# A hybrid decoder step on one core: where the extra weight slots live, and the order of two sets of output projections

## The chip, the cores and the metric

The kernel runs on one core of a Trainium2 chip. The metric is the device time of one execution in microseconds. The median of three runs before the change is 1149.12 us (1148.29 to 1151.05). The engines are called as in the profile: PE is the matmul engine and PEld its weight load, DVE the vector engine, ACT the scalar engine, POOL the GpSimd engine, and SP the queue that issues most transfers.

## The reference, cut to what matters

Two layers of a decoder run on 512 prompt tokens and 8 sampled tokens, all in float32:

```
for i in range(2):
    if i == 0:  m = attention(x)      # q,k,v projection, sliding window 128, sinks, then @ w_o
    else:       m = gated_linear_attention(x)   # q,k,v,gate, 4 heads, then @ w_o
    x = layer_norm(ALPHA * x + m)
    h = x @ w_up[i]; a, u = halves of h
    y = (gelu(causal_conv3(a)) * u) @ w_down[i]
    x = layer_norm(ALPHA * x + y)
```

Beside x, the kernel returns the new key and value windows, the new GLA states (for each of the 8 samples and 4 heads a 128x256 matrix, decayed and updated with an outer product), and the new convolution rows.

## The kernel before, in words

**Groups and units.** The 520 tokens are two groups: A has 256 columns, B has 264 (256 prompt and the 8 samples). All activations lie transposed, features on the partitions. The weights are cut into 187 units of up to 128 output columns (`plan`): 10 for q, k, v; 8 for the attention's output projection; 68 for the first feed-forward (44 up, 24 down in three parts); 25 for the GLA (a rank-16 projection and six per head); 8 for its output projection; 68 for the second feed-forward. So there are six phases, in this order. Each unit is used twice, once for A and once for B. Such a use is called a product here, and A3 is the product of group A with the fourth unit of the phase at hand.

**Precision.** A float32 product is made of three reduced-precision ones. `load_unit` (L147) brings a unit in with one DMA into `raw` (two buffers), ACT copies it into a high part `wh` (L158), DVE subtracts to get the low part `wl` (L161). `product` (L164) then runs 24 matmuls: for each of eight 128-row chunks `wh` times the activations' high part, `wh` times their low part, and `wl` times the high part. In most of the feed-forward, group A uses a wider form with the same work (`product2`, L178). Products are summed in four PSUM buffers (`accp`).

**Slots.** `wh` and `wl` live in slots. Six are there all the time (`WSLOTS`). When B has used a unit, its slot takes the next unit that is not yet loaded (`next_unit`), so a unit that takes over a slot can't be converted before that B product has read the old one. One more slot (`EXTRA`) is a pool of its own. It is opened when a feed-forward begins and closed near its end; it takes no new unit among the last eight of a layer (`XEND`). Pools lie on a stack: a pool that is opened takes the memory of the pools closed before it.

**Order.** `order` gives the program order of products. A runs ahead of B, by a number of products from `LEADS`. In the output projections it gives

```
layer 0   A0 A1 A2 A3 A4 A5 B0 A6 B1 B2 A7 B3 B4 B5 B6 B7
layer 1   A0 A1 A2 A3 A4 B0 A5 B1 A6 B2 A7 B3 B4 B5 B6 B7
```

and a feed-forward begins A0 to A5, B0, A6, B1, B2, A7, B3, A8, B4, and so on in turn, and ends A67, B63, B64, B65, B66, B67. That is program order. The order on each engine is made by a scheduler, which runs the program in a timing model of its own and gives each engine what is ready there, earlier work first. `issue_after` and `keep_in_program_order` add edges that fix the order of two instructions on one engine.

**After a product.** An output projection adds its result to x (L219) and feeds the running sums of a layer norm (`ln_chunk`). Behind the eighth, `ln_end` finishes the norm: column sums by matmuls with `ones_a` (L256), a few rows of statistics on DVE and ACT, eight subtractions of the mean, most on POOL (L263), and then for each chunk a multiplication on DVE (`u`, L296), the high part on ACT (L297), x itself on POOL (L298), and the low part on DVE (L301). The next phase's products of this group read these parts.

**The mixers' ends.** Sampled tokens have steps of their own, spawned with a delay counted in products (`spawn`, `due`). `attn_sample` ends three products after B9 of the attention, and closes the attention's pool. `gla_sample` for the last head starts its state updates five products after that head's last value product: four steps, one product apart, each with a DMA that spreads two rows of v over all partitions (`vb`, L840, one buffer), two ACT multiplications (L844), two DVE updates (L845) and a DMA that writes the state out (L846). In program order the last of them stands nine products after that value product, at A5 of the output projection, and there the GLA's pool is closed. The next pool's tiles are `sconv`, `aext` and others of the feed-forward (`ffn_open`), or those of the GLA (`gla_open`).

Of the kernel before, what the change touches and what calls it, by code (L numbers as in the profile page):

```python
# [37 lines left out]


LAG = 4  # L40
LEADS = (4, 5, 5, 5, 4, 5)

WSLOTS = 6
RAWS = 2
HIACT = 2

EXTRA = 1
XEND = 8
ACCS = 4

WARM = 8
# [40 lines left out]
class Net:  # L92
    def __init__(self, tc, ctx, I, O):
# [38 lines left out]
            g.hl = self.act.tile(s, F32R, name=f"hl_{g.name}")  # L132
        self.units = []
        self.w = {}


    def open(self, name, bufs=1):
# [26 lines left out]
    def product(self, g, u, rh, rl):  # L164
        nc = self.nc
        h, l = self.w[u]
        nt = self.units[u][1]
        ps = self.acc.tile([P, 512], F32, name="accp")
        o = ps[:, :g.n].rearrange("p (j t) -> p j t", t=2)
        for k in range(nt):  # L170
            ks = slice(k * P, (k + 1) * P)
            xh, xl = in_turn(rh[:, k]), in_turn(rl[:, k])
            nc.tensor.matmul(o, h[:, ks], xh, start=k == 0, stop=False)  # L173
            nc.tensor.matmul(o, h[:, ks], xl, start=False, stop=False)  # L174
            nc.tensor.matmul(o, l[:, ks], xh, start=False, stop=k == nt - 1)  # L175
        return ps[:, :g.n]

    def product2(self, g, u, rs, rh, rl, wide):  # L178
# [320 lines left out]
    def attn_sample(self, g):  # L499
# [27 lines left out]
        for v in range(2):  # L527
            own = slice(64 * v, 64 * v + 64)
            src = pv[own, :P].rearrange("p (b h) -> p h b", h=16)[:, 8 * v:8 * v + 8]
            for t in range(2):  # L530
                self.split(g.hh[own, :, t, P:], g.hl[own, :, t, P:], src[:, :, t::2])
        self.close(self.ap_cm)


    def out_proj(self, g, u, m, i):
# [5 lines left out]

    def ffn_open(self, layer):
        nc = self.nc
        if EXTRA:
            self.wx, self.wx_cm = self.open(f"wts{layer}", EXTRA)
        self.fp, self.fp_cm = self.open(f"ffn{layer}")
        p = self.fp
        self.sconv = p.tile([P, NF, NS, 2], F32, name="sconv")
# [256 lines left out]
    def gla_sample(self, g, h, q, k, v0, v1, ep, kraw):  # L805
# [42 lines left out]
                g.st.append(self.state_load(h + 1, p))  # L848
        if h == GH - 1:
            self.close(self.gp_cm)  # L850

    def gla_g(self, g, u, h, i):
        nc, n = self.nc, g.n
# [77 lines left out]
    def order(self):  # L931

        out, n = [], len(self.units)
        for p0, p1, top in zip(self.phases, self.phases[1:] + [n], LEADS):
            b = p0
            for u in range(p0, p1):
                out.append((0, u))
                lead = max(LAG, min(top, p0 + 2 * top - u))
                if u < LAG:
                    lead = LAG - 1  # L940
                while b <= u - lead:
                    out.append((1, b))
                    b += 1
            out += [(1, u) for u in range(b, p1)]
        return out

    def more(self, u):

        end = self.phases[3] if u < self.phases[3] else len(self.units)
        return self.nu < end - XEND  # L950

    def next_unit(self, extra):
        u = self.nu
# [6 lines left out]
    def run(self):  # L960
        nc = self.nc
        self.plan()
        self.nu, self.extra, self.close_wx = WSLOTS, {}, False
        self.attn_open()
        self.later, self.slot, self.seq, self.pool_mark = [], 0, 0, None
        for i, u in self.order():
            g = self.groups[i]
            _, _, f, a, pre = self.units[u]
            if i == 0 and pre:
                pre()  # L970
                if pre != self.gla_open:
                    for _ in range(EXTRA):
                        self.next_unit(True)
            self.slot += 1
            self.resume(f(g, u, *a))
            if i == 1:
                x = self.extra.pop(u, False)
                if not x or self.more(u):
                    self.next_unit(x)
                elif not self.extra:  # L980
                    self.close_wx = True
            if self.close_wx and self.fp is None:
                self.close(self.wx_cm)
                self.close_wx = False
            self.due()
        while self.later:
            self.slot += 1
            self.due()
# [115 lines left out]
```

## Time and profile before

| | |
|---|---|
| median of the runs | 1149.12 us (1148.29 to 1151.05) |
| profiled execution | 1146.73 us, of which the span from first to last instruction is 1144.7 us |
| PE, PEld busy | 1104.2 us (96%), 1055.2 us (92%) |
| DVE, ACT, POOL busy | 794.5 us (69%), 575.6 us (50%), 326.4 us (29%) |
| DMA | 122.82 MB, mean 107 GB/s |
| mean granted PE clock | 0.992 of full |

The phases lie about so in the span: attention to 133 us, its output projection mostly to 168 us, first feed-forward to 529 us, GLA to 734 us, its output projection to 767 us, second feed-forward to 1129 us, and the last norm and the output to the end. An instruction's row in the timeline has its start, its length, engine and line, what it writes and reads, its shape, and in brackets the engine's idle time before it with what ended it. A row of windows has for each engine its busy time and, in brackets, its instructions, then the granted clock, the DMA's share and its rate.

### The profile page before, as it was taken

Reading aid. Unit: us, or ns where it says so; the run is one execution under the profiler, and the core shown is the slowest. Engines: PE = TensorE matmul, PEld = TensorE weight load, DVE = VectorE, ACT = ScalarE, POOL = GpSimd, SP = SyncE. Lnnn points to the kernel's source line nnn. Section 1 sums busy time; section 2 is a strip of 40 time slices with the busy share of each in tenths; the row PEclk is TensorE's granted clock in tenths of the full one; section 3 lists DMA queues with packets and bytes.
Section 4 is the critical chain, followed back from the end, with each engine's and each line's share of the span. In section 5 each row is a group of like instructions: output and inputs, shape, how many; then the busy total and the mean of one; then the engine's idle time right before and its main releaser. Section 6 shows DMA issues by size and latency. Waiting matters only on the chain.

```text
span 1144.7 us, 22953 instructions
## 1 busy us (share of the span) xinstructions
PE 1104.2 (96%) x8806; PEld 1055.2 (92%) x8806; DVE 794.5 (69%) x1663; ACT 575.6 (50%) x1253; POOL 326.4 (29%) x556
## 2 busy tenths in 40 slices
PE   8999899999999999999899999989999999999995
PEld 8997798999999999998899999888999999999994
DVE  7897589655665566668867777799655665566657
ACT  5677457534553245435545556456524553245433
POOL 4575568100110011357300101287100110011344
PEclk9999999999999999999899999999999999999998
DMA  7553031323323233243124355341333232232222
GB/s 241 149 183 90 13 111 56 111 93 123 99 93 111 92 99 105 74 133 110 38 89 147 117 177 162 133 145 62 105 96 127 93 106 98 92 111 93 74 63 75
DMA packets 53789, 122.82 MB, mean 107 GB/s; under 512 B 6792, under 2 KB 27312, under 8 KB 53680
## 3 DMA queue, kind: packets, MB, share of 16 engines
q1 hardware_dynamic: 51664, 119.61, 32.4%
q10 hardware_dynamic: 2016, 1.75, 0.5%
q8 instruction: 69, 1.13, 0.4%
q14 instruction: 40, 0.33, 0.1%
HBM read 108.67 MB, written 8.47 MB: 102 GB/s over the span
## 4 chain that ended last, share of the span: by engine, by line
PE 70%; DVE 12%; DMA 6%; ACT 4%; POOL 4%; issue 4%; SPq 0%; ACTq 0%; DVEq 0%; POOLq 0%
PE accp L191 15%; PE accp L174 14%; PE accp L173 14%; PE accp L175 14%; PE accp L192 8%; DMA vb<-dv 3%; DVE wl L161 2%; POOL x_b L298 1%; DVE sgla L845 1%; DMA qs<-hl 1%; ACT wh L158 1%; POOL x_a L298 1%; DVE u L296 1%; PE pv L494 1%; DVE msq L276 1%
## 5 line engine op out<-in xcount | busy, mean ns | idle before, releaser
L161 DVE TENSOR_TENSOR wl<-raw,wh 128x1024 fp32r<-128x1024 f32 (+2 forms) x189 | 231.4, 1226 | 106.7 <-ACT wh L158 105.2
L158 ACT ACTIVATE wh<-raw 128x1024 fp32r<-128x1024 f32 (+2 forms) x185 | 191.9, 1037 | 215.0 <-PE accp L174 196.8
L173 PE MATMUL accp<-xh_b,wh 128*128 128x264 f32 x976 | 271.7, 279 | 2.5 <-DVE hprod L600 2.5
L174 PE MATMUL accp<-xl_b,wh 128*128 128x264 f32 x976 | 271.3, 278 | 0.2
L175 PE MATMUL accp<-xh_b,wl 128*128 128x264 f32 x976 | 270.8, 278 | 0.0
L191 PE MATMUL accp<-xs_a,wh 128*128 128x512 f32 x576 | 196.3, 382 | 0.0
L173 PEld LDWEIGHTS accp<-xh_b,wh 128*128 128x128 f32 x976 | 185.0, 190 | 3.5 <-DVE hprod L600 2.9
L174 PEld LDWEIGHTS accp<-xl_b,wh 128*128 128x128 f32 x976 | 184.9, 189 | 3.1 <-DVE xl_b L301 0.6
L175 PEld LDWEIGHTS accp<-xh_b,wl 128*128 128x128 f32 x976 | 184.8, 189 | 0.8 <-issue 0.6
L192 PE MATMUL accp<-xs_a,wl 128*128 128x256 f32 x576 | 145.4, 273 | 0.0
L173 PE MATMUL accp<-hh_b,wh 128*128 128x264 f32 x480 | 133.7, 279 | 3.3 <-ACT hh_b L198 3.3
L174 PE MATMUL accp<-hl_b,wh 128*128 128x264 f32 x480 | 134.3, 280 | 0.0
L175 PE MATMUL accp<-hh_b,wl 128*128 128x264 f32 x480 | 133.3, 278 | 0.0
L191 PEld LDWEIGHTS accp<-xs_a,wh 128*128 128x128 f32 x576 | 109.1, 189 | 11.4
L173 PE MATMUL accp<-xs_a,wh 128*128 128x256 f32 x400 | 112.3, 287 | 5.6 <-DVE x_b L219 2.1
L174 PE MATMUL accp<-xs_a,wh 128*128 128x256 f32 x400 | 112.4, 283 | 3.2 <-DVE xs_a L301 2.9
L192 PEld LDWEIGHTS accp<-xs_a,wl 128*128 128x128 f32 x576 | 110.2, 191 | 1.9
L175 PE MATMUL accp<-xs_a,wl 128*128 128x256 f32 x400 | 111.0, 280 | 0.7 <-DVE wl L161 0.5
L173 PEld LDWEIGHTS accp<-hh_b,wh 128*128 128x128 f32 x480 | 91.3, 190 | 3.8 <-ACT hh_b L198 3.6
L174 PEld LDWEIGHTS accp<-hl_b,wh 128*128 128x128 f32 x480 | 91.3, 190 | 1.4 <-issue 0.3
L175 PEld LDWEIGHTS accp<-hh_b,wl 128*128 128x128 f32 x480 | 91.3, 190 | 0.2
L202 POOL COPY hist<-aext 128x2 f32<-128x2 f32 x44 | 8.9, 203 | 284.4 <-DVE aext L578 281.3
(320 smaller groups left out, 2495.3 us busy)
## 6 DMA issues: line engine op xcount, KB each, us to landing
raw<-in_w_up SPq DMA_DIRECT2D x88, 512.0 KB, 3.4
raw<-in_w_down SPq DMA_DIRECT2D x32, 512.0 KB, 3.4
raw<-in_w_gla SPq DMA_DIRECT2D x24, 512.0 KB, 3.4
raw<-in_w_mix_o SPq DMA_DIRECT2D x16, 512.0 KB, 4.1
raw<-in_w_down SPq DMA_DIRECT2D x16, 384.0 KB, 3.1
qs<-hl SPq DMA_DIRECT2D x64, 64.0 KB, 2.1
sgla<-in_state_gla SPq DMA_DIRECT2D x16, 256.0 KB, 2.8
vb<-dv SPq DMA_DIRECT2D x16, 256.0 KB, 3.7
```

Source lines behind the costliest of these rows:

```text
L158: nc.scalar.activation(h[:, c], r[:, c], AF.Copy)
L161: nc.vector.tensor_tensor(l[:, c], r[:, c], h[:, c].bitcast(F32), op=ALU.subtract)
L173: nc.tensor.matmul(o, h[:, ks], xh, start=k == 0, stop=False)
L174: nc.tensor.matmul(o, h[:, ks], xl, start=False, stop=False)
L175: nc.tensor.matmul(o, l[:, ks], xh, start=False, stop=k == nt - 1)
L191: both = lambda: nc.tensor.matmul(o, h[:, ks], in_turn(rs[:, k].rearrange("p t q j -> p t (q j)")), start=k == 0, stop=last)
L192: low = lambda: nc.tensor.matmul(o[:, :P], l[:, ks], in_turn(rh[:, k]), start=False, stop=False)
L276: nc.vector.scalar_tensor_tensor(q, q, 0.5, nv, op0=ALU.mult, op1=ALU.mult)
L296: nc.vector.tensor_tensor(u, x[:, m], r, op=ALU.mult)
L298: ts = nc.gpsimd.tensor_scalar(x[:, m], u, sc(m), bi(m), op0=ALU.mult, op1=ALU.add)
L494: mm = nc.tensor.matmul(pv[64 * v:64 * v + 64, b * P:(b + 1) * P], self.vtok[:, kb, 64 * v:64 * v + 64], parts[v][w][:, b], start=i == 0, ...
L845: late(nc.vector.scalar_tensor_tensor(s[:, j], vb[:, j], kraw[:, b:b + 1], s[:, j], op0=ALU.mult, op1=ALU.add))
```

## The change

The four slots take the place of the one. They are opened when a mixer closes its pool, inside the projections, instead of at the feed-forward's start, and keep taking units to the layer's end. `order` is changed in four of the six phases. In the output projections it now gives

```
layer 0   A0 A1 A2 A3 A4 A5 B0 A6 A7 B1 B2 B3 B4 B5 B6 B7
layer 1   A0 A1 A2 A3 A4 A5 B0 B1 A6 A7 B2 B3 B4 B5 B6 B7
```

and a feed-forward begins A0 to A6, B0, A7, B1, A8, B2 and ends A67, B61 to B67. In the projections each product's first matmul is queued behind the last one of the product before it, so PE runs them in program order, and the first product of the feed-forward too. Other matmuls may still come between.

With the program's own counting of slots, the new pool opens in layer 0 at A2, and takes A6, A7 and the feed-forward's first two units. In layer 1 it opens at B0 (nine products after the value product in the new order), whose own slot has just taken A6's unit, and takes A7 and the feed-forward's first three.

```diff
-LEADS = (4, 5, 5, 5, 4, 5)
+LEADS = (4, 5, 6, 5, 4, 6)
...
-EXTRA = 1
-XEND = 8
+EXTRA = 4
+XEND = 0
...
+        self.last_mm = None
...
-            nc.tensor.matmul(o, h[:, ks], xh, start=k == 0, stop=False)
+            with self.tc.issue_after(self.last_mm) if k == 0 and self.last_mm else ExitStack():
+                nc.tensor.matmul(o, h[:, ks], xh, start=k == 0, stop=False)
             nc.tensor.matmul(o, h[:, ks], xl, start=False, stop=False)
-            nc.tensor.matmul(o, l[:, ks], xh, start=False, stop=k == nt - 1)
+            mm = nc.tensor.matmul(o, l[:, ks], xh, start=False, stop=k == nt - 1)
+        self.last_mm = mm.ins if self.chained(u) else None
...
         self.close(self.ap_cm)
+        self.open_extra()
...
-        if EXTRA:
-            self.wx, self.wx_cm = self.open(f"wts{layer}", EXTRA)
...
             self.close(self.gp_cm)
+            self.open_extra()
...
-        for p0, p1, top in zip(self.phases, self.phases[1:] + [n], LEADS):
+        for i, (p0, p1) in enumerate(zip(self.phases, self.phases[1:] + [n])):
             b = p0
             for u in range(p0, p1):
                 out.append((0, u))
-                lead = max(LAG, min(top, p0 + 2 * top - u))
-                if u < LAG:
-                    lead = LAG - 1
+                if i in (0, 3):
+                    top = LEADS[i]
+                    lead = max(LAG, min(top, p0 + 2 * top - u))
+                    if u < LAG:
+                        lead = LAG - 1
+                elif i in (2, 5):
+                    lead = LEADS[i]
+                else:
+                    lead = LEADS[i] if u == p0 + WSLOTS - 1 else NF
...
+    def chained(self, u):
+        return any(self.phases[i] <= u < self.phases[i + 1] for i in (1, 4))
...
+    def open_extra(self):
+        self.wx, self.wx_cm = self.open(f"wx{self.nu}", EXTRA)
+        for _ in range(EXTRA):
+            self.next_unit(True)
...
-                if pre != self.gla_open:
-                    for _ in range(EXTRA):
-                        self.next_unit(True)
```

## The prediction

> **What bounds the kernel now.** I read the page for shares first, then windows to find where PE idles, then PE's waits for the reason.
>
> ```profile
> PE 1104.2 (96%) x8806; PEld 1055.2 (92%) x8806; DVE 794.5 (69%) x1663; ACT 575.6 (50%) x1253; POOL 326.4 (29%) x556
> ```
>
> ```profile
> core 0: us, PE busy (x) PEld busy (x) DVE busy (x) ACT busy (x) POOL busy (x), PEclk, DMA share, GB/s
> 200.00:520.00 320.00, 320.00 (x2477) 309.19 (x2476) 194.79 (x363) 142.85 (x259) 49.13 (x131) 1.00 0.32 103
> 160.00:200.00 40.00, 35.90 (x303) 34.59 (x302) 37.17 (x75) 25.97 (x48) 31.89 (x35) 1.00 0.24 78
> 520.00:545.00 25.00, 22.51 (x190) 21.77 (x189) 23.62 (x45) 13.24 (x24) 19.92 (x18) 1.00 0.32 106
> 548.60:558.10 9.50, 6.29 (x26) 4.68 (x26) 7.81 (x22) 5.91 (x12) 5.00 (x6) 0.74 0.00 1
> 553.10:560.00 6.90, 6.31 (x23) 5.11 (x24) 4.57 (x14) 4.05 (x8) 0.95 (x2) 0.51 0.07 15
> 739.00:800.00 61.00, 55.30 (x465) 53.56 (x465) 55.77 (x106) 38.36 (x71) 46.94 (x52) 1.00 0.32 103
> 136.70:140.10 3.40, 3.40 (x23) 3.07 (x20) 1.26 (x3) 0.78 (x2) 0.14 (x2) 0.50 0.22 55
> ```
>
> ```profile
> PE accp L173 <- ACT hh_b L198: 3.3, 2, 2.7
> PE accp L174 <- DVE xs_a L301: 2.9, 2, 1.5
> PE accp L173 <- DVE hprod L600: 2.5, 2, 1.3
> PE accp L173 <- DVE x_b L219: 2.1, 2, 1.1
> ```
>
> PE bounds it, and inside a feed-forward it never stops (320.00 us of 320). So more slots and a longer lead can bring nothing there; the change lives in the turns between phases. Each of them is short of cover: group A's norm, and then B's, isn't done when PE wants its chunks, and DVE (37.17 us of 40) is what runs late. Idle PE is 4.10 us in the first turn (160 to 200), 2.49 and 3.21 us in the turn into the GLA, 5.70 us in the turn out of it (739 to 800). The waits name the norm's low parts (L301), PSUM buffers that a busy DVE frees late (L600, L219) and B's last mixer chunk (L198). Two stretches run at half clock, one behind the 2.7 us wait for L198, one at the GLA's start.
>
> **First turn (attention, projection, feed-forward).** The new slots need the attention's memory. When that comes free can be seen at the feed-forward's `aext`, whose pool lies in the same memory:
>
> ```profile
> 137.87 0.14 POOL L571 MEMSET aext<- 128x2 f32 x2 [1.22 <-PE pv L494]
> ...
> 752.46 0.14 POOL L571 MEMSET aext<- 128x2 f32 x2
> ```
>
> ```profile
> 750.00 0.39 SPq L846 DMA_DIRECT2D out_gla_s<-sgla  x1
> ```
>
> Its clearing waits for nothing of its own, and yet starts as the attention's last matmul ends (137.8), and in layer 1 some 2.4 us after the last state is sent out. Both look like the end of the whole old pool, so I take it that a new pool waits for that.
>
> ```profile
> 141.66 1.06 ACT L158 ACTIVATE wh<-raw 128x1024 fp32r<-128x1024 f32 x1 [3.43 <-PE accp L174]
> ```
>
> ```profile
> 153.63 0.28 PE L173 MATMUL accp<-hh_b,wh 128*128 128x264 f32 x1
> ```
>
> B0 is read to its end at 141.6; A6's conversion now starts there. In the new order A6 and A7 find slots free from 137.9; two conversions of ACT (1.06 us each) and DVE (1.23 us) are done by about 141.5, under B0. A7 then ends at 141.6 + 2 x 2.7 = 147.0 instead of 153.6 (where B3 begins), 6.6 us earlier, and 7 products instead of 5 cover A's norm. The 4.10 us and a further 0.5 us before B's mean should nearly all go. Against it stand three more units converted (12, for B0 to B7 and four new slots, instead of 9) in this stretch: 3 x 1.23 = 3.7 us of a DVE that has no room. Bounds: a gain of 4.6 us if all stalls go, 0.9 if those 3.7 us come back in full; DVE's backlog is cleared 6.6 us sooner, so I stay near the first: **-4.0**. The 2.7 us wait for L198 and its half clock stay, since B0 keeps its place.
>
> **Second turn (feed-forward, GLA).** A67 ends two products (5.4 us) sooner, so A's norm does, and the 2.49 us go. B's norm is queued behind A's on POOL, and its last chunk comes out late:
>
> ```profile
> 540.34 0.75 POOL L263 TENSOR_TENSOR x_b<-x_b,mu 128x264 f32<-128x264 f32 x1
> ```
>
> ```profile
> 554.46 0.43 DVE L301 TENSOR_TENSOR xl_b<-x_b,xh_b 128x264 fp32r<-128x264 f32 x1
> ```
>
> ```profile
> 549.76 0.38 PE L671 MATMUL accp<-xh_b,wh 128*128 128x264 f32 x1 [1.13 <-ACT v_a L739]
> ```
>
> Moved by 5.4 us, that chunk is there at 549.5. PE reaches B's rank product at 549.76 - 1.13 - 2.49 = 546.1 and has 1.8 us of work in it, so it still idles some 2 us rather than 3.2, and the half clock behind (6.9 us at 0.51, at most 3.4 us lost) may come or not: I take half of it, 1.7. Together -2.5 - 1.2 - 1.7 and a little for the GLA's decay chain, which starts sooner too: **-6.0**, with bounds -2.5 (B's part unchanged) and -9.1 (2.49 + 3.21 + 3.4). `gla_open` moves from 498.0 to where B79, the last product out of the extra slots, ends, about 512.5:
>
> ```profile
> L630 POOL MEMSET reset<- x1: 318/318/318, 498.0 to 498.0; 128x264 f32 x1
> ```
>
> Its clearings on POOL and two DMAs on ACT's queue then meet A's mean subtraction. They are some 2 us, under the 5.4 us gained; without that cover they would cost those 2.
>
> **Third turn (GLA, projection, feed-forward).** Here the chained order meets the pool's end.
>
> ```profile
> 744.04 0.27 PE L173 MATMUL accp<-hs_a,wh 128*128 128x256 f32 x1
> ...
> 749.42 0.27 PE L173 MATMUL accp<-hs_a,wh 128*128 128x256 f32 x1
> ...
> 752.10 0.28 PE L173 MATMUL accp<-hh_b,wh 128*128 128x264 f32 x1
> ...
> 767.39 0.49 PE L173 MATMUL accp<-xs_a,wh 128*128 128x256 f32 x2 [0.76 <-ACT xs_a L297]
> ```
>
> ```profile
> 741.89 1.22 DVE L161 TENSOR_TENSOR wl<-raw,wh 128x1024 fp32r<-128x1024 f32 x1
> 743.03 0.88 DVE L845 SCALAR_TENSOR_TENSOR sgla<-vb,kraw,sgla 128x256 f32<-128x256 f32 x2
> ...
> 748.60 1.37 DVE L845 SCALAR_TENSOR_TENSOR sgla<-vb,kraw,sgla 128x256 f32<-128x256 f32 x2 [0.50 <-issue]
> ...
> 780.61 0.97 DVE L301 TENSOR_TENSOR xs_a<-x_a,xs_a 128x256 fp32r<-128x256 f32 x1 [0.38 <-POOL x_a L298]
> ```
>
> ```profile
> DMA to landing us min/median/max: 3.0/3.7/5.0
> ```
>
> The last row is that of `vb`. A0 to A5, B0 and B1 end at 744.0 (A6's first matmul), 743.5 without the 0.6 us wait for L198, which A5 now fills. A6 sits in B0's old slot and ends at 743.5 + 2.7 = 746.2 (A7 shows 2.7 us: 749.42 to 752.10). A7's unit is in an extra slot, free only when the last state has landed, 752.4 now. That chain is four steps of a 3.7 us DMA and its update, and isn't touched; its third step loses the 0.8 us that it now waits behind a weight split (741.89), so 751.6. Conversion takes 1.06 us on ACT to A7's first matmul (752.7), DVE another 1.2 to its third (753.9). PE idles 746.2 to 752.7 and one more us: 7.5 us, and because products are chained no B product may pass. ACT and DVE queue A7's conversion too, but hold only sums for B's norm behind it. After 2.7 us of idle PE lost half of 3.40 us (136.7 to 140.1), so I add 1.7. A7 then ends at 753.9 + 2.5 + 1.7 = 758.1, 6.0 us late, and one more product follows it: the feed-forward starts 6.0 + 2.7 = 8.7 us later. A's last low part, 29 us behind A7 (752.3 to 781.6), is then 3 us nearer to that start, so of this turn's 5.1 us of stalls behind 766 (5.70 less 0.6) I take 3.6 as gone: 8.7 - 3.6 = **+5.1**. Bounds: -4.0 if nothing holds A7 (the 0.6 us and the 3.4 us of A's norm go), and +14.3 if `vb` takes 5.0 us three times (+3.9), the clock stays down 6.9 us (+1.7) and none of the stalls goes (+3.6).
>
> Trainium skill, "TensorE: Matmul & The Clock Gate", part 1, "What's actually happening", speaks against this turn: PE's clock falls to half after an idle window of about 3.4 us and rises after a busy one as long. By that rule the 6.5 us of waiting are sure to bring the half clock, where the trace brought it after only 2.7; the sum is the same by both.
>
> **End of the kernel.** A67 ends 5.4 us sooner, which frees DVE for B's last chunks and takes this wait, **-0.3** (0 to -0.5):
>
> ```profile
> 1129.66 0.46 PE L256 MATMUL tp<-s_b,ones_a 128*128 128x264 f32 x1 [0.32 <-ACT sq L237]
> ```
>
> `XEND` 0 and longer leads inside a feed-forward: 0, under 320 us of unbroken PE; were that cover gone, one conversion (1.06 + 1.22 us) each time.
>
> **Sum.** -4.0 - 6.0 + 5.1 - 0.3 = -5.2 us on the profiled execution's 1146.7, its span plus 2.0 around it, so 1141.5. The median stands 2.4 us higher, and moves alike: 1149.1 - 5.2 = **1143.9**.
>
> **The rivals.**
>
> *Nothing holds A7.* The scheduler might place the state chain earlier, or a slot might wait only for the tiles under it. For it: the GLA's pool is larger than four slots. Against it: `aext` and the attention's end, on two layers. Then the third turn is -4.0 and the sum -14.3: 1134.8.
>
> *DVE keeps the gain.* Conversions brought forward fill what the earlier norm frees: first turn -0.9, second -2.5. For it: 37.17 us of 40 busy. Against it: the scheduler puts earlier work first, and the norm of A stands ahead of most loads. Sum +1.4, so 1150.5, no change that can be told.
>
> *The chained A7 outweighs the rest.* One place, PE between A6 and A7 in layer 1. From 10.3 us on it eats the other terms, from 13.7 us on the kernel is slower by 0.3%. At its upper bound of 14.3 the sum is +4.0: 1153.1. For it: transfers of weights run while `vb` is fetched, and 5.0 us have been seen. Against it: the median of 3.7.
>
> *Chaining does nothing*, because the order is the program's already: PE now puts a piece of B0 among A5's (the wait for L198 shows between them), so it does something, if little; the sum would keep everything but the 0.6 us: 1144.5.
>
> **How the numbers follow.** Chances: forecast 0.48 (its own range 1140.5 to 1147.5), A7 not held 0.12, DVE keeps the gain 0.24, A7 outweighs 0.16 (the chaining that does nothing lies in the forecast). About 0.3%, 3.4 us, is what a measurement can tell: faster is below 1145.7. That takes 0.42 of the forecast and all of the first rival, 0.54; slower, above 1152.5, is the last, 0.16; the rest 0.30. The range reaches from 1137.5, which leaves out most of the first rival, to 1153.5, which leaves out the upper half of the last.
>
> **What would show it.** First turn: A7 done near 147, idle PE from 160 to 200 under 1 us. Second: no wait for L301 before the rank product, and the clock after the GLA's start above 0.9. Third: `aext`'s clearing or the first extra conversion near 752, PE idle some 6 us ahead of it, a slice at half clock behind, B2 to B7 without stop. I am wrong if A7 of layer 1 starts by 748, if the first turn's waits for L301 or L600 are still there, or if the feed-forwards show idle PE.

## The result, and the profile after

The changed kernel takes 1156.43 us in the median (1155.49 to 1157.13), the kernel before, on the same chip, 1149.14: a ratio of 1.0064, 95% interval 1.005 to 1.0078. It is 7.3 us slower; 1143.9 had been forecast. The profiled execution took 1155.49 us (span 1153.6), 8.8 us more than the one before.

First the page's shares and the view of windows, for the changed kernel. The columns of a window are its length, and for each engine the busy time and its instructions, then the granted clock and the transfers.

```profile
PE 1106.2 (96%) x8806; PEld 1054.9 (91%) x8806; DVE 792.7 (69%) x1663; ACT 574.0 (50%) x1253; POOL 321.6 (28%) x556
```

```profile
200.00:520.00 320.00, 319.90 (x2472) 308.86 (x2470) 192.51 (x364) 140.73 (x257) 47.92 (x127) 1.00 0.30 96
160.00:200.00 40.00, 37.24 (x302) 35.98 (x301) 35.77 (x74) 23.86 (x44) 29.07 (x32) 0.96 0.25 80
553.10:560.00 6.90, 5.25 (x28) 4.05 (x29) 5.96 (x20) 5.62 (x13) 3.08 (x5) 1.00 0.00 1
739.00:800.00 61.00, 48.74 (x380) 45.70 (x378) 48.50 (x92) 33.02 (x58) 37.71 (x44) 0.94 0.42 129
751.70:758.60 6.90, 4.15 (x18) 3.89 (x19) 4.08 (x6) 3.97 (x5) 4.12 (x8) 0.51 0.47 142
```

PE's work is the same, its busy time 2.0 us longer. Inside the feed-forward it still never stops. From 160 to 200 us it idles 2.76 us instead of 4.10. The half clock at the GLA's start has gone (1.00 where 0.51 stood). But the turn out of the GLA (739 to 800) now has 12.3 us of idle PE instead of 5.7, and 6.9 us at half clock, where it had none.

PE's longest waits in the changed kernel (microseconds in all, times, longest):

```profile
PE accp L175 <- ACT wh L159: 6.8, 3, 6.0
PE accp L176 <- DVE xs_a L305: 2.7, 4, 1.0
PE accp L175 <- DVE hprod L603: 2.3, 1, 2.3
```

The first is new. It is A7 of layer 1, in the rows of the timeline around it (PE, ACT, SP's queue and DVE):

```profile
747.70 0.28 PE L177 MATMUL accp<-hs_a,wl 128*128 128x256 f32 x1
754.00 0.55 PE L175 MATMUL accp<-hs_a,wh 128*128 128x256 f32 x1 [6.03 <-ACT wh L159]
...
752.85 1.06 ACT L159 ACTIVATE wh<-raw 128x1024 fp32r<-128x1024 f32 x1 [0.77 <-DMA out_gla_s<-sgla]
...
743.85 0.46 SPq L843 DMA_DIRECT2D vb<-dv  x1
750.36 0.39 SPq L849 DMA_DIRECT2D out_gla_s<-sgla  x1
...
748.50 1.84 DVE L848 SCALAR_TENSOR_TENSOR sgla<-vb,kraw,sgla 128x256 f32<-128x256 f32 x2 [3.30 <-issue]
```

The last fetch of `vb` is issued at 743.85, its update starts at 748.50, the state goes out at 750.36, and only when that transfer is done does ACT convert A7's weights into the slot (752.85). PE stands still for 6.03 us.

**Where the time went.** I cut the trace at four matmuls that both kernels have: the first of B0 in the first projection, the last of the first feed-forward, the last of B's products of the GLA's first head, and the last of the GLA's. In the changed kernel these are the rows

```profile
136.78 0.38 PE L175 MATMUL accp<-hh_b,wh 128*128 128x264 f32 x1 [1.15 <-ACT hh_b L202]
...
531.25 0.28 PE L177 MATMUL accp<-hh_b,wl 128*128 128x264 f32 x1
...
597.79 0.28 PE L177 MATMUL accp<-xh_b,wl 128*128 128x264 f32 x1
...
712.85 0.28 PE L177 MATMUL accp<-xh_b,wl 128*128 128x264 f32 x1
...
1139.98 0.61 PE L262 MATMUL pv<-sq,ones_a 128*128 128x264 f32 x2
```

and PE's work between two cuts is nearly the same, so their distances can be compared. Each stretch runs to the end of its last matmul (us; the third turn reaches to PE's last matmul, and so holds the end of the kernel too):

| | median | first turn | second | GLA | third |
|---|---|---|---|---|---|
| before | 1149.1 | 392.9 | 70.2 | 115.2 | 417.5 |
| changed | 1156.4 | 394.7 | 66.5 | 115.1 | 427.5 |

In these two traces the first turn lost 1.8 us, the second gained 3.7, the third lost 10.0. Idle PE in the three turns was 4.6, 5.7 and 6.2 us and is 5.3, 4.7 and 13.0 now; half clock, at half of its length, cost 1.7, 3.4 and 0 us and costs 1.7, 0 and 3.4 now. The rest, 0.9 us, is the attention; over the traces below, B0 starts between 135.5 and 137.6 us also where nothing ahead of it was touched, and the GLA's stretch varies from 113.8 to 116.3 (c2 aside). One trace's stretch is good to about 1 us, and what is said of the turns rests on several. A trace is also one execution, and its time can stand 2.6 us off the median beside it (the one before the change is 2.4 us under its median), so the stretches of a row need not add up to its median.

### The profile page after: what moved, and what is told of

Read it like the earlier page. It is cut to its first block, busy times and chain, and to the rows that moved or that the text cites. A ratio compares the mean times of both kernels' runs of the same rounds, so it can differ in the third digit from the quotient of the medians.

```text
span 1153.6 us, 22939 instructions
## 1 busy us (share of the span) xinstructions
PE 1106.2 (96%) x8806; PEld 1054.9 (91%) x8806; DVE 792.7 (69%) x1663; ACT 574.0 (50%) x1253; POOL 321.6 (28%) x556
## 5 line engine op out<-in xcount | busy, mean ns | idle before, releaser
L162 DVE TENSOR_TENSOR wl<-raw,wh 128x1024 fp32r<-128x1024 f32 (+2 forms) x189 | 228.6, 1212 | 112.5 <-ACT wh L159 111.1
L195 PEld LDWEIGHTS accp<-xs_a,wh 128*128 128x128 f32 x576 | 109.1, 189 | 11.4
L175 PEld LDWEIGHTS accp<-xs_a,wh 128*128 128x128 f32 x400 | 76.2, 194 | 7.8 <-DVE hprod L603 2.5
```

Source lines behind the costliest of these rows:

```text
L162: nc.vector.tensor_tensor(l[:, c], r[:, c], h[:, c].bitcast(F32), op=ALU.subtract)
L195: both = lambda: nc.tensor.matmul(o, h[:, ks], in_turn(rs[:, k].rearrange("p t q j -> p t (q j)")), start=k == 0, stop=last)
```

## The experiments

Three theories stood at the start. Theory 1: the third turn's loss is A7 of layer 1, whose slot comes free only with the GLA's memory. Theory 2: the first turn's gain is eaten by the conversions for three more units, which DVE makes inside A's norm. Theory 3: it is eaten by the chaining. The stretches of all runs, cut at the same matmuls:

| run | what it is | median | first | second | GLA | third |
|---|---|---|---|---|---|---|
| a1 | changed, no chaining | 1159.3 | 394.5 | 66.5 | 116.3 | 429.6 |
| a2 | before, four slots alone | 1168.3 | 403.8 | 68.4 | 114.8 | 430.1 |
| a3 | changed, A7 of layer 1 in B1's slot | 1151.6 | 394.0 | 66.3 | 114.3 | 422.7 |
| a4 | before, chaining alone | 1150.7 | 392.8 | 69.9 | 113.8 | 419.9 |
| b1 | before, flat lead of six, two slots | 1150.0 | 395.7 | 66.6 | 115.2 | 421.8 |
| b2 | changed, A7 of layer 1 behind B3 | 1156.5 | 393.3 | 66.0 | 114.4 | 429.9 |
| b3 | changed, two slots | 1157.4 | 394.6 | 68.7 | 114.7 | 424.6 |
| b4 | changed, no last state update | 1144.3 | 393.7 | 66.3 | 116.0 | 417.1 |
| c1 | before, late lead of six | 1147.1 | 393.6 | 68.6 | 115.5 | 418.5 |
| c2 | before, late lead of eight | 1175.0 | 394.3 | 73.5 | 132.5 | 424.1 |
| c3 | before, late lead of five | 1144.4 | 392.9 | 67.0 | 114.7 | 418.2 |
| c4 | changed in layer 0 alone | 1146.2 | 392.7 | 68.6 | 114.5 | 419.5 |
| d1 | c4, late lead of six | 1146.6 | 393.9 | 66.1 | 114.6 | 419.0 |
| d2 | d1 with two slots | 1149.3 | 394.3 | 68.6 | 115.8 | 418.8 |
| d3 | c4 with two slots | 1152.1 | 396.1 | 68.6 | 114.4 | 418.8 |
| d4 | two slots, late lead of five | 1145.7 | 394.3 | 66.6 | 115.1 | 417.5 |
| e1 | d2, first Gelu behind B's norm | 1144.6 | 390.9 | 68.6 | 114.3 | 419.1 |
| e2 | d4, first Gelu behind B's norm | 1142.4 | 391.0 | 67.4 | 114.2 | 417.8 |

### The third turn

**Without the last state update (b4).**

```diff
+            if h == GH - 1:
+                yield 1
+                nc.sync.dma_start(out=self.O["gla_s"][2 * p:2 * p + 2, h].rearrange("b k v -> k b v"), in_=s)
+                continue
             vb = self.gp.tile([P, 2, 256], F32, name="vb")
```

> The changed kernel without the last head's update of the sample states: its four fetches of vb, eight scalings on ACT and eight multiply-adds on DVE are left out, and the states go out as they were read. So the GLA's memory comes free without that chain. Theory 1: A7's weights are converted some 10 us earlier, no idle PE ahead of A7, no half clock: 1156.4 - 6.0 - 3.4 - 0.5 = 1146.5, and about 1 us less for 8 x 0.8 us of DVE: 1145 to 1147. Rival (A's norm sets the turn): half of the wait comes back as idle PE behind B7, 1150 or more.

The kernel leaves out that update, so it is of use for its time alone. Measured: 1144.33 us, 12.1 under the changed kernel and 2 under what was expected. Its windows:

```profile
739.00:800.00 61.00, 57.21 (x481) 55.16 (x480) 54.31 (x101) 38.30 (x68) 46.33 (x49) 1.00 0.33 107
748.00:760.00 12.00, 11.41 (x97) 11.11 (x97) 11.28 (x16) 7.75 (x14) 10.78 (x10) 1.00 0.45 152
```

The idle PE falls from 12.3 to 3.8 us and the half clock goes. Theory 1 holds for the cause. But the third turn is 417.1 us, 0.4 under the kernel before: with nothing holding A7, and eight updates less to do, the new order and the four slots bring this turn nothing that a trace can tell.

**A7 in a slot of its own (a3).** The extra slots are opened when A7's unit has taken B1's slot.

```diff
             self.close(self.gp_cm)
-            self.open_extra()
+            self.held = True
...
             self.due()
+            if self.held and self.nu >= self.phases[5]:
+                self.open_extra()
+                self.held = False
```

> The changed kernel, but in layer 1 the extra slots are opened only when A7's unit has taken the slot that B1 frees, so they hold units of the feed-forward alone. Theory 1: A7 follows A6 near 748 without the 6.0 us wait and the half clock behind it; 6.0 + 3.4 + 0.5 us go: 1156.4 - 9.9 = 1146.5 (1144 to 1149). Rival (A's norm sets the start of the feed-forward in any case): the idle PE moves behind 766, where A's low parts come out, and 1152 or more is left. In the first turn nothing changes.

Measured: 1151.59 us (ratio to before 1.0018, 1.0008 to 1.0028). The 6.0 us wait for the slot went, and 3.9 us of it came back at once (PE and DVE rows):

```profile
750.34 0.38 PE L177 MATMUL accp<-hs_a,wl 128*128 128x256 f32 x1 [3.88 <-DVE wl L162]
...
747.18 1.42 DVE L848 SCALAR_TENSOR_TENSOR sgla<-vb,kraw,sgla 128x256 f32<-128x256 f32 x2 [3.72 <-issue]
748.53 1.76 DVE L162 TENSOR_TENSOR wl<-raw,wh 128x1024 fp32r<-128x1024 f32 x1
```

A7's high part is there, but its low part is queued on DVE behind the last state update, and DVE stands still for 3.72 us ahead of that. The profile names no releaser for this wait ("issue"); that it is the fetch of `vb`, issued at 742.12, is read from the step before it, whose 1.44 us of waiting the trace puts down to that fetch by name. It is the same chain, met at another place: neither theory nor rival had it there. In the kernel before, that update came with 0.50 us of waiting, since conversions and sums filled the time.

**A7 behind B3 (b2).**

```diff
-LEADS = (4, 5, 6, 5, 4, 6)
+LEADS = (4, 5, 6, 5, 2, 6)
```

> The changed kernel with A6 and A7 of layer 1 behind B3 instead of behind B1; A7 stays in the slot that waits for the GLA's memory. Theory 1: PE reaches A7 two products later, 748.0 + 5.4 = 753.4, and the weights are there at 754.0: under 1 us of idle PE and no half clock, 1156.4 - 5.4 - 3.4 = 1147.6, less what A's norm gives back, as A7 still ends some 4 us later than before: 1148 to 1151. Rival (what PE waits for is a step of its own that shifts with the order, such as the sums for B's chunks): a wait of 3 us or more remains ahead of A7, 1153 to 1156.

Measured: 1156.51 us, nothing gained. Ahead of A7 only 1.8 us of waits are left, as theory 1 had it, but they stand elsewhere:

```profile
PE accp L175 <- ACT xs_a L301: 6.8, 2, 5.4
...
PE accp L175 <- ACT wh L159: 1.8, 3, 1.0
```

PE now waits 5.4 us at the feed-forward's start for A's norm. What sets this turn here is the chain from A7's weights through A7 to the norm of A; covering the first wait with B's products only moves the idle time to the chain's end, and 6.8 us at half clock go with it (from 774.5).

**Without chaining (a1), and chaining alone (a4).** The first edit is a1's, to the changed kernel; the second a4's, to the kernel before, with `chained` as in the change.

```diff
-        return any(self.phases[i] <= u < self.phases[i + 1] for i in (1, 4))
+        return False
```

```diff
-            nc.tensor.matmul(o, h[:, ks], xh, start=k == 0, stop=False)
+            with self.tc.issue_after(self.last_mm) if k == 0 and self.last_mm else ExitStack():
+                nc.tensor.matmul(o, h[:, ks], xh, start=k == 0, stop=False)
```

> The changed kernel without the chaining of the projections' products, nothing else. Theory 1 (A7 of layer 1 sits in a slot that comes free only with the GLA's memory): in the PE order that comes out, two matmuls of A7 still stand ahead of B2, so PE waits for A7's converted weights as before, about 6 us, with a slice at half clock behind: layer 1 unchanged, 1156.4 us. Theory 2 (the loss of the first turn comes from three more units converted on DVE inside A's norm): first turn unchanged too, 1156.4 together. Theory 3 (the loss of the first turn comes from the chained A products): 1156.4 - 2.7 = 1153.7. Rival to 1 (it is the chaining that keeps PE from working past A7): the 6 us and the half clock go, 1147 to 1150.

> The kernel before with the chaining of the projections' products alone; slots, order and leads as before. Theory 3 (chaining costs the first turn, as the A products no longer fill the attention): +1 to +3, 1150.1 to 1152.1, with A0 of the first projection ending near 110 us and attention ending some 1 us later. Theories 1 and 2 alone: within 0.3% of 1149.1, and slightly under it (0.6 us) in layer 1, where PE no longer waits for B's last mixer chunk inside B0.

Measured: a1 1159.31 us, still with a wait of 6.04 us for A7's weights, since two matmuls of A7 stand ahead of B2 in PE's order anyway; the first turn is 394.5 as in the changed kernel. That is 2.9 us more than theory 1 had expected: PE then waits another 5.2 us for A's norm (781.4). a4 1150.74 us (ratio 1.0018, 1.0004 to 1.0031), with a first turn of 392.8 and a third of 419.9. Theory 3 falls, and so does the name of my rival, "the chained A7": the slot holds A7, with or without the chain.

**The slots alone (a2).** The kernel before with the new slots; order and leads as before.

```diff
-EXTRA = 1
-XEND = 8
+EXTRA = 4
+XEND = 0
...
         self.close(self.ap_cm)
+        self.open_extra()
...
             self.close(self.gp_cm)
+            self.open_extra()
```

> The kernel before with the four extra slots opened at the end of a mixer and used to the end; order, leads and the free PE order as before. Theory 1: A7 of layer 1 is in an extra slot here too, but stands behind B2; PE reaches it near 749.4 and waits to about 753.6, 4 us, with or without a half-clock slice of 3.4 us: third turn +4 to +7.5. Theory 2: first turn +1 to +3. Together 1149.1 + 5.7 + 2 = 1157, at least 1153. Theory 3 without 2: 1149.1 + 5.7 = 1155. Rival (the new order is to blame, not the slots): 1149 to 1150, and no wait for A7's weights.

Measured: 1168.27 us, worse than the whole change by 12 us, and 11 more than expected. The first and third turn lose 11 and 13 us:

```profile
PE accp L175 <- ACT xs_a L301: 7.2, 2, 6.9
PE tp L260 <- DVE s_b L251: 7.2, 1, 7.2
PE accp L175 <- ACT wh L159: 5.2, 3, 4.4
```

With A7 at its old place and three units more to convert, A's norm comes 7 us later in the first turn, and PE waits for it. So the slots cost. In the first turn the changed kernel, with its new order and lead, gets 9.1 of those 10.9 us back, in the third only 2.6 of 12.6.

### The first turn

In the changed kernel A7 ends 5 us earlier (148.8 against 153.8), but A's norm does not. DVE between A7 and A's last low part, in the kernel before:

```profile
153.83 0.42 DVE L219 SCALAR_TENSOR_TENSOR x_a<-x_a,accp 128x256 f32<-128x256 f32 x1
...
157.51 1.23 DVE L161 TENSOR_TENSOR wl<-raw,wh 128x1024 fp32r<-128x1024 f32 x1
...
162.86 1.75 DVE L161 TENSOR_TENSOR wl<-raw,wh 128x1024 fp32r<-128x1024 f32 x1
...
166.22 0.76 DVE L296 TENSOR_TENSOR u<-x_a,r 128x256 f32<-128x256 f32 x2
...
180.93 0.96 DVE L301 TENSOR_TENSOR xs_a<-x_a,xs_a 128x256 fp32r<-128x256 f32 x1 [0.38 <-POOL x_a L298]
```

and in the changed one:

```profile
151.69 0.41 DVE L223 SCALAR_TENSOR_TENSOR x_a<-x_a,accp 128x256 f32<-128x256 f32 x1
...
152.58 1.76 DVE L162 TENSOR_TENSOR wl<-raw,wh 128x1024 fp32r<-128x1024 f32 x1
...
156.04 1.21 DVE L162 TENSOR_TENSOR wl<-raw,wh 128x1024 fp32r<-128x1024 f32 x1
...
159.02 1.69 DVE L162 TENSOR_TENSOR wl<-raw,wh 128x1024 fp32r<-128x1024 f32 x1
...
165.37 1.21 DVE L162 TENSOR_TENSOR wl<-raw,wh 128x1024 fp32r<-128x1024 f32 x1
166.50 0.75 DVE L300 TENSOR_TENSOR u<-x_a,r 128x256 f32<-128x256 f32 x2
...
181.93 0.42 DVE L305 TENSOR_TENSOR xs_a<-x_a,xs_a 128x256 fp32r<-128x256 f32 x1
```

A7's sum is taken 2.9 us after its product ended. Between that sum and the norm's first multiplication (`u`) stand four weight splits (`wl`) instead of two, and up to the last low part eight instead of six, so this stretch takes 30.7 us instead of 28.1. The multiplication comes at 166.5, where it came at 166.2, and the last low part ends at 182.4, 0.5 us later than before: A7 ends 5.0 us sooner, and 2.9 and 2.6 us are lost behind it. The splits for A6 and A7 (139.59 to 141.95) also stand ahead of B's last mixer part, for which PE now waits 1.1 us inside B0 (142.46).

**Two slots (b3), and the parts against each other (c4, d1, d2, d3).** b3 is the changed kernel with `EXTRA` 2. c4 is the change in layer 0 alone, with the second layer as before (first edit, cut); d1 begins the feed-forward with the old lead and takes six from its 21st unit on (second); d2 and d3 are d1 and c4 with two slots.

```diff
-LEADS = (4, 5, 6, 5, 4, 6)
+LEADS = (4, 5, 6, 5, 4, 5)
...
             self.close(self.gp_cm)
-            self.open_extra()
...
-                if i in (0, 3):
+                if i in (0, 3, 4, 5):
...
-        return any(self.phases[i] <= u < self.phases[i + 1] for i in (1, 4))
+        return any(self.phases[i] <= u < self.phases[i + 1] for i in (1,))
```

```diff
-                    lead = LEADS[i]
+                    lead = max(LAG, min(5, p0 + 10 - u)) if u < p0 + 20 else LEADS[i]
```

> The changed kernel with two extra slots instead of four: in the first turn they hold A6 and A7, in the other turn A7 and the feed-forward's first unit; all else alike. Theory 2 (conversions inside A's norm): ten instead of twelve, 2 x 1.23 us of DVE less; first turn's +2.7 falls to about +0.2; third turn keeps the 6 us wait: 1156.4 - 2.5 = 1153.9, down to 1151 if the third turn gains as much. Rival (what delays A's norm is its place in program order, not the count of conversions): 1156.

> The change in the first layer alone (four slots from the attention's end, A6 and A7 ahead of B1, chained products, flat lead of six); from the GLA's projection on all is as in the kernel before. By the times of the traces from B0 on, the first turn is +1.0 (0.3 to 1.8 in the four runs that have it) and the second -3.7: 1149.1 - 2.7 = 1146.4 (1145 to 1148). If the first turn's loss were larger than these traces show, as theory 2 first had it (+2.7): 1148.1. If the third turn as before has a loss of its own in the changed kernel's time: 1149 or more.

> The run of the first layer alone (1146.2 us, four slots, flat lead of six), with the feed-forward begun with the lead of the kernel before (five, then four) and six only from its 21st unit on. Theory 5 (the sixth product of A ahead of B0 finds no chunk and no PSUM buffer of its own and delays B's norm): 1146.2 - 2 = 1144.2. Theory 2 alone (four slots' conversions): no change, 1146.2.

> As four slots with the late lead, but with two extra slots (they hold A6 and A7 of the first projection, so two conversions fewer stand inside A's norm). If both theories hold, the first turn gains what was forecast of it, some 3 to 4 us: 1149.1 - 3.7 - 3 = 1142.4 (1141 to 1144). Theory 2 alone: 1146.2 less up to 2; theory 5 alone: as with four slots.

> The run of the first layer alone with two extra slots instead of four, flat lead of six. Theory 2 alone: A's norm ends near 177, 1146.2 - 2 = 1144. Theory 5 (the flat lead eats it): A's norm ends near 177 too, and the time stays at 1146 or above, as in the run of the whole change with two slots.

Measured: b3 1157.38, c4 1146.16, d1 1146.58, d2 1149.29, d3 1152.06 us. (b3 keeps the 6.0 us wait for A7 of layer 1.) The half of the change that c4 keeps is a gain, ratio 0.9973 (0.9961 to 0.9984). Its time came out as expected, its parts did not: -0.2 and -1.6 us in its trace, where +1.0 and -3.7 had been put. Theory 5, that the sixth product of A delays B's norm, falls with four slots, as d1 is no faster than c4; with two, the flat lead costs 2.8 us (d3 against d2).

Two slots take two conversions out of A's norm, and the norm does what theory 2 says: in d2 it has six splits again and takes 27.6 us from A7's sum, and its last low part starts at 176.50 (first row below), 5.4 us earlier than with four. Yet the medians with two slots are not lower than those with four. Part of that is the second turn, where d2 has 6.8 us at half clock and d1 none; but d2's first turn (394.3) is not shorter than d1's (393.9) either. What eats the earlier norm there is on ACT:

```profile
176.50 0.42 DVE L305 TENSOR_TENSOR xs_a<-x_a,xs_a 128x256 fp32r<-128x256 f32 x1
...
180.69 1.28 ACT L591 ACT_TABLE_LOAD   x1
181.98 0.42 ACT L591 ACTIVATE conv<-conv 128x256 f32<-128x256 f32 x1
182.41 1.28 ACT L277 ACT_TABLE_LOAD   x1
...
184.15 1.28 ACT L278 ACT_TABLE_LOAD   x1
...
190.57 0.38 PE L175 MATMUL accp<-xh_b,wh 128*128 128x264 f32 x1 [2.75 <-ACT xh_b L301]
```

A's norm is early, so A's first feed-forward products are too, and their first Gelu (L591) runs between the sums of B's norm and its logarithm (L277). ACT loads the Gelu's function table, then one for the logarithm, one for the exponential, and at 186.32 the Gelu's again: four loads where the kernel before has one. b3 and d3 have the same four. B's norm is late, and PE waits 2.75 us for its first chunk.

**The Gelu behind B's norm (e1).** d2 with the first Gelu of A ordered behind B's exponential, whose norm is for that emitted one product earlier.

```diff
-        yield 1
+        if not g.i or i % 2:
+            yield 1
...
-        nc.scalar.activation(r, r, AF.Exp, scale=-0.5)
+        self.exp_mark = nc.scalar.activation(r, r, AF.Exp, scale=-0.5).ins
...
-        nc.scalar.activation(c[:, :n], c[:, :n], AF.Gelu)
+        with self.tc.issue_after(self.exp_mark) if j == 0 and g.i == 0 else ExitStack():
+            nc.scalar.activation(c[:, :n], c[:, :n], AF.Gelu)
```

> The run with two slots in the first layer and a late lead of six (1149.3 us), with the feed-forward's first Gelu of A ordered behind the exponential of B's norm. Theory 6 (the early Gelu makes ACT swap tables inside B's norm): one table load instead of four, 3 x 1.28 = 3.8 us off B's norm, so the 2.75 us of idle PE ahead of B0 and the half-clock slice behind it (1.7 us) go: 1149.3 - 4.4 = 1144.9 (1144 to 1146.5). Rival (B's norm is late for DVE's sake): unchanged, 1148 to 1150.

Measured: 1144.63 us, 4.7 under d2. The first turn is 390.9, 3.4 shorter, and its ACT rows are

```profile
180.44 0.44 ACT L278 ACTIVATE r<-nv 128x264 f32<-128x264 f32 x1
180.91 0.42 ACT L279 ACTIVATE r<-r 128x264 f32<-128x264 f32 x1
181.35 1.28 ACT L593 ACT_TABLE_LOAD   x1
```

One table load, as before. The edit has two parts, and the trace tells them apart: the sums of B's norm start 42.2 us behind B0's first matmul in d2 and in e1 alike, so emitting the norm earlier did not move them; the exponential behind them ends 4.5 us earlier.

This first turn, and that of e2 with 391.0, are the only ones of the study that are shorter than the old one beyond what traces differ by: -2.0 us, by two slots, A7 ahead of B1, and the Gelu held back, together. Most of it is the clock: the 3.4 us at half clock of the old turn (from 136.7), worth 1.7 us, are not in these two traces, while idle PE fell by 0.9 us, from 4.6 to 3.7. Of what is left, 1.1 us is the wait inside B0 and 1.9 us are waits for A's low parts.

### The second turn

**The lead alone (b1, c1, c2, c3).** b1 is the kernel before with a flat lead of six in the feed-forward and two extra slots at its start. c1 and c2 take the lead of six or eight only from the 21st unit on, and fill the slots they need beyond the first at the 13th (the edit below, with the lead 6, 8 or 5). c3 keeps the lead of five to the end and uses the one old slot to the end (`XEND` 0).

```diff
                 lead = max(LAG, min(top, p0 + 2 * top - u))
+                if i in (2, 5) and u >= p0 + 20:
+                    lead = 5
...
+            if i == 1 and u - 12 in (self.phases[2], self.phases[5]):
+                for _ in range(EXTRA - EARLY):
+                    self.next_unit(True)
```

> The kernel before with the feed-forward's lead of six alone: two extra slots opened where the one was (at the feed-forward's start), used to the end; projections and mixers as before. It has the change's second turn without its first and third. If the gain of the second turn (3.6 us by the times of B's last product of the feed-forward and of the GLA's first head) hangs on the lead alone: 1149.2 - 3.6 + about 1 us for one more conversion at each projection = 1146.6. If it hung on the four slots or on A6 and A7 being earlier: 1149 to 1151.

> The kernel before, with the lead of six only from the feed-forward's 21st unit on, and a second extra slot that is filled at its 13th unit, where PE never stops. Start of the feed-forward, projections and mixers as before. Theory 4 (the second turn's 3.7 us hang on the lead at the end of the feed-forward alone, and the lead of six with one more conversion at its start is what cost the run with lead six alone its gain): 1149.1 - 3.7 = 1145.4 (1144 to 1147). Rival (the gain needs the longer lead all along, or what is gained is given back at the GLA): 1149 to 1150.

> As the run with the late lead of six, but with four extra slots, three of them filled at the 13th unit, and a lead of eight from the 21st on. A67 then ends two products (5.4 us) sooner still. Theory 4: the idle time that is left in the turn into the GLA (4.7 us in the changed kernel, of which about 2 us are B's chunks, that hang on B's last product and not on A's) shrinks by 1 to 3 us more: 1142.5 to 1145. Rival (B's norm, which no lead of A moves, is all that is left): as with six, 1145.4.

> The kernel before, with the lead of five kept up to the feed-forward's end (it falls to four behind the sixth unit there) and the one extra slot used to the end: no slot more than before. Theory 4: one product instead of two ahead of A's norm covers 2.7 of the 5.4 us; A's wait of 2.5 us goes, B's stays: 1149.1 - 2.5 = 1146.6. Rival: 1149 to 1150.

Measured: b1 1150.04, c1 1147.13, c2 1175.02, c3 1144.39 us. b1 has the gain in the second turn (66.6) and gives it back in the other two (395.7 and 421.8); c1, which begins the feed-forwards as before, loses less there (393.6 and 418.5). c1's ratio is 0.9981 (0.9973 to 0.999), a little over its expected range. c3, which needs no slot more than the kernel before, has most of that gain (67.0), ratio 0.9964 (0.995 to 0.9977). With the lead of six the second turn takes 66.0 to 66.6 us in the seven traces without a half-clock slice there (the changed kernel, a1, a3, b1, b2, b4, d1), and 68.6 to 68.7 in the six with 6.8 us of it (b3, c1, c4, d2, d3, e1). So most of what separates them is the clock. Why a longer lead does not always avoid the slices stays open. c3, with one slice of 3.4 us, gets its gain from idle PE: 5.7 us in this turn before, 3.2 in c3.

c2 I had wrong by 30 us. Its second turn and its GLA are 3 and 17 us longer, and ACT shows why (timeline, then the group with the most loads):

```profile
500.46 1.28 ACT L241 ACT_TABLE_LOAD   x1
...
504.10 1.28 ACT L589 ACT_TABLE_LOAD   x1 [0.48 <-issue]
505.39 0.43 ACT L589 ACTIVATE conv<-conv 128x264 f32<-128x264 f32 x1
...
509.44 1.28 ACT L274 ACT_TABLE_LOAD   x1
...
511.48 1.28 ACT L275 ACT_TABLE_LOAD   x1
```

```profile
L799 ACT ACT_TABLE_LOAD x12 | 15.4, 1283 | 1.8 <-DVE gsmall L798 1.6
```

The program preloads a table that serves logarithm and exponential with the sums of A's seventh chunk (L241). With A eight products ahead, that comes before B's last Gelu, which loads its own table over it. From there on a change from logarithm to exponential or back mostly brings a load, through the whole GLA: 44 loads from 505 to 760 us, 57 in this execution against 7 in the kernel before. That these loads are what cost the time is argued from the trace; no run has the lead of eight without them.

**The gains together (d4, e2).** d4 is two slots in layer 0 with the late lead of five in both feed-forwards; e2 is d4 with the Gelu of e1. Beside d2, d4 has the edit below; its last line lets layer 1's one extra slot take units to the end, as in c3.

```diff
-LEADS = (4, 5, 6, 5, 4, 5)
+LEADS = (4, 5, 5, 5, 4, 5)
...
+                    if i == 5 and u >= p0 + 20:
+                        lead = LEADS[i]
...
-        return self.nu < end - (XEND if u < self.phases[3] else 8)
+        return self.nu < end - XEND
```

> Two extra slots in the first layer with A6 and A7 ahead of B1, the lead of the kernel before at the start of each feed-forward and five from its 21st unit on; the second layer's projection as before. The run with the late lead of five alone took 1144.4; if the first turn's gain of 3 us adds to that: 1141.4. If B's norm takes that gain: 1144.4.

> The same order of the Gelu in the run with two slots and a late lead of five (1145.7 us). Theory 6: 1145.7 - 4.4 = 1141.3, under every kernel so far. Rival: 1145 to 1146.

Measured: d4 1145.68 us, nearest to its second case (1144.4); the four table loads are in it too. e2 1142.35 us (1140.04 to 1143.71), ratio 0.9941 (0.9925 to 0.9957): 7.0 us under the kernel before and 14 under the changed one. The window of its turn into the GLA:

```profile
520.00:545.00 25.00, 24.74 (x209) 24.06 (x208) 22.32 (x47) 15.36 (x28) 17.61 (x25) 1.00 0.37 125
```

From 520 to 545 us PE idles 0.3 us instead of 2.5. The third turn is left as it was before.

## Why the prediction was wrong, step by step

**First turn, forecast -4.0, measured +1.8 (between -0.2 and +1.8 in the five traces that have the same first turn: changed, a3, b2, b4, c4).** The traces that begin with the old first turn (before, c1, c2, c3) take 392.9 to 394.3 themselves, so a loss is not shown; what is shown is that the gain of 4.0 did not come. That A6 and A7 come earlier was right; A7 ended at 148.8, forecast 147.0. The step that failed is "DVE's backlog is cleared 6.6 us sooner, so I stay near the first". In the order that DVE was given, the three extra splits do not fill its gaps: one stands ahead of A7's sum, two between the steps of A's norm, and its last low part comes 0.5 us later than before. So PE still waits for A's chunks (1.8 and 0.7 us at 172.6 and 173.7), which the prediction had named as a sign of being wrong. "The 2.7 us wait for L198 and its half clock stay" was wrong too: the wait fell to 1.15 us, with no half clock behind it (it is 2.75 in a1, without the chaining); the slice came behind A's chunks instead. The lower bound, a gain of 0.9, was the better of the two and still not reached. Behind it lay a limit that I had not priced: B's norm, which needs B7 (its last matmul ended at 168.2 us before, about 170 in the changed kernel), wherever A7 ends. It showed when A's norm did come early (b3, d2, d3), and only e1 and e2 got 2 us out of this turn.

**Second turn, forecast -6.0, measured -3.7.** Inside its bounds, in part by luck. The clock term was too small (1.7 taken; all of the 3.4 us came, as the clock stayed at 1.00, which it does not in every trace with this lead), the idle term too large: 3.7 us were to go, and 1.0 went. A67 did end sooner, 5.8 us by the end of the feed-forward's last product (528.8 before, 531.5 now), and A's first low part came 5.1 us sooner, but its last only 3.1, and PE still waits for A's low parts (2.4 us for L305, where L301 had 1.4). The step that failed is that B's chunk is "moved by 5.4 us" with A's norm: its last low part

```profile
557.50 0.42 DVE L305 TENSOR_TENSOR xl_b<-x_b,xh_b 128x264 fp32r<-128x264 f32 x1
```

ends 26.4 us behind that product, where it was 26.1.

**Third turn, forecast +5.1, measured +10.0.** The mechanism was right to the row: the slot waits for the last state (752.9; forecast 751.6), idle PE 6.03 + 0.45 us ahead of A7 (forecast 7.5), A7's end 759.5 (forecast 758.1). Two sizes were off, both named in the upper bound: the half clock lasted 6.9 us, not 3.4 (+1.7), and none of the old stalls went ("I take 3.6 as gone": outside the wait for A7, idle PE from 735 to 810 us was 5.8 us, where all of it had been 5.7). The lower bound's -4.0 was wrong too: without the holder (b4) the turn gains 0.4.

**End and inside of the feed-forward.** The wait at the end is gone, too small to tell in time; PE is busy 319.9 of 320 us: both right.

**Sum and rivals.** -5.2 became +7.3. Of the rivals, "DVE keeps the gain" was right for the first turn, and "the chained A7 outweighs the rest" for the sign. I had it decide only from 13.7 us on, since I counted on 10 us of gains; with 2 us of gains, 10.0 were enough. Its name was wrong, as a1 shows.

## What to carry to other kernels

A chain is shortened only if what else its engines do is moved out of it: weights loaded earlier are also conversions made earlier, and in the engine's order they can come between the steps of whatever is running there. When a memory pool is reopened for weights, what holds it is the last user's whole chain, its fetches, updates and writes, so put into it what is needed last; and if covering a wait moves it downstream (b2), the chain and not the order is the limit. Before moving work across phases, list the function tables that ACT uses in each: in d2 one Gelu out of place took back what the earlier norm had brought. The cheapest variant here (c3) only raises the lead from four to five late in each feed-forward and uses its one slot to the end; the best (e2) adds to that two slots, a new order and chaining in layer 0 and one ordering edge, for 2 us more, and the intervals of their ratios overlap.

## What the runs showed of the hardware

**Function tables.** A table load took 1.28 us each time. Its cost lies in where it falls: taking three of them out of B's norm brought 4.7 us (e1 against d2) and 3.3 (e2 against d4) by the medians, 3.3 to 3.4 in the first turn of the traces; c2, with fifty more, most of them around the GLA, took 26 us more. The Trainium skill, "ScalarE: Activation LUTs", "Table sets: the hidden batching unit", says that functions are loaded as sets and that one set has both logarithm and exponential. The traces agree only while that set, preloaded, stays in: once a Gelu had replaced it, a logarithm and the exponential behind it brought a load each (d2, 182.41 and 184.15).

**The clock.** Half-clock slices lasted 3.4 us or a multiple, as at 751.7 to 758.6. The Trainium skill, "TensorE: Matmul & The Clock Gate", part 1, "What's actually happening", has a free-running window of that length and an idle window ahead of the drop. The length agrees; but the changed kernel also had such a slice from 174.9 to 178.3 us behind two waits of only 1.8 and 0.7 us, which the runs here don't explain. c4 has the same two waits (1.8 and 0.7 us) and no slice behind them. If the window runs freely, a wait is sure to hold a whole one only from twice its length on, by estimate 6.8 us, so the prediction's "sure" for 6.5 us went too far, though the slice came.
